# Layer-1 ConvFFN: an up projection as a 2x2 block product of seven products, then a separate down projection

## The chip, the cores and the metric

The kernel runs on one core of one Trainium2 chip. The metric is the device time of one execution in microseconds (us), given as the median of several runs. TensorE (PE) does the matmuls, VectorE (DVE), ScalarE (ACT) and GpSimd (POOL) work on tiles in SBUF and PSUM, and SyncE (SP) issues nearly all transfers from and to DRAM.

## The reference

A network of two layers on 1024 latent tokens and 256 context tokens with 1024 features: differential attention in layer 0, 2-D neighbourhood attention in layer 1, and behind each a gated convolutional FFN with 2816 hidden features. The FFN of layer 1 works on the 1024 latent tokens alone:

```python
def conv_ffn(t, w_up, w_conv, b_conv, w_down):
    u = t @ w_up                                   # 1024 -> 2 x 2816
    up = jnp.pad(u, ((0, 0), (1, 1), (0, 0)))
    acc = b_conv
    for tap in range(3):
        acc = acc + up[:, tap:tap + n] * w_conv[tap]
    a, g = jnp.split(acc, 2, axis=-1)
    return (jax.nn.silu(g) * a) @ w_down           # 2816 -> 1024
...
h2 = rmsnorm(x, norm_ffn[i]) * (1.0 + sc2) + sh2
x = x + g2 * conv_ffn(h2, ffn_up[i], ffn_conv[i], ffn_conv_b[i], ffn_down[i])
...
return rmsnorm(x, norm_out)
```

## The kernel before

Everything is float32. A matmul operand is kept as two rounded parts, high and low, and a product is three matmuls: high by high, high weight by low token, low weight by high token. Features lie on the 128 partitions, tokens on the free axis, so 1024 features are 8 chunks (kc) and 1024 tokens are two blocks of 512 columns, the width of one matmul and of one PSUM bank. H[b] is a pair of tiles, Hh and Hl, the normalised tokens of block b.

Weights come through one object, `W`. Its queue names every weight tile in the order of use, and `get()` keeps four of them made ahead. For each, `load` issues a 512 KB transfer into one of three raw tiles (line 106, on SP), lets POOL round it to the high part (`tensor_scalar`, L115) and subtract for the low part (`tensor_tensor`, L117), into one of five split slots (wsp). A slot is free again when its last matmul is done.

`wo_proj` (L397) is the output projection of the attention. At each block's end DVE adds it to the residual X (L406), ACT squares it (L298) and DVE sums the squares into SS (L299). `rnorm` (L302) makes the factor R of a block: eight matmuls on SS (L306), a root on ACT, a reciprocal, a product with the identity on DVE (L312), two matmuls that spread it (L315) and a copy on ACT (L316). `norm_mod` (L319) writes t, Hh and Hl from it (L328 DVE, L329 ACT, L330 DVE). The norm of block 1 is made inside the first up products.

`ffn(1, ...)` then goes over 22 units i of 128 hidden features. Per unit the up product takes two weight tiles, a and g, over both token blocks (`gemm`, L345): 2 x 8 chunks x 3 x 2 blocks = 96 matmuls. `conv` reads the sum u from PSUM: ACT makes the middle tap (L458), DVE the two others (L463); ACT makes the SiLU (L521), `gate` multiplies (DVE L471), rounds (ACT L472) and subtracts (DVE L473). The down product of an earlier unit is laid between the up products of the next ones: `down_step` takes 48 matmuls a unit (L488), and for every output chunk and block DVE adds the result to X in SBUF (L489). Each sum there is three matmuls, so L489 runs 16 times a unit, 352 in all. The last block's sums of squares and output are written at the end: `finish1`, `write`.

A scheduler sets the order on each engine from the program's order and its data dependences; no table of numbers touches this change.

## Time and profile before

| | us |
|---|---|
| median of 3 runs (lowest to highest) | 3350.94 (3348.80 to 3353.13) |
| the profiled execution, its own time | 3355.75 |
| its span, first to last instruction | 3354.0 |
| PE busy in it | 3234.7 |
| DVE busy | 2213.5 |
| POOL busy | 1169.2 |
| layer-1 FFN, first up to last down matmul | 2600.4 to 3335.6 |

The span is what lies between the first and the last instruction; the execution's own time lies 1.75 us over it. The rows below are cut from this one execution. In them a busy time is the sum over the instructions of an engine, "xN" is a count of instructions, and an arrow "<-" behind an idle time names what ended it. L numbers are lines of the kernel before.

### The profile page before, as it was taken

To read this page: it belongs to the slowest core of one execution; us is meant where nothing else is said; L and a number is where in the kernel's file an instruction comes from. 1 tells how busy PE (TensorE), PEld (TensorE's weight loads), DVE (VectorE), ACT (ScalarE), POOL (GpSimd) and SP (SyncE) were. 2 spreads that over 40 slices of the span, in tenths; PEclk is the share of its full clock that TensorE was granted. 3 is DMA by queue.
4 is the path that set the end of the run, shared out by engine and by line. 5 is a ranking of instruction groups with operands and counts; after the bars stand their busy time and mean duration, and the time that the engine had idled before them with its cause. 6 is when DMAs were issued, how large, how long until landed. Compare 5 with 4: busy or idle time off the path is not lost.

```text
span 3354.0 us, 42504 instructions
## 1 busy us (share of the span) xinstructions
PE 3234.7 (96%) x16160; PEld 2675.9 (80%) x16160; DVE 2213.5 (66%) x3647; ACT 1027.7 (31%) x1796; POOL 1169.2 (35%) x793
## 2 busy tenths in 40 slices
...
GB/s 261 160 210 169 126 112 106 114 116 71 142 69 52 46 55 44 52 50 51 51 38 38 32 116 262 238 126 199 198 157 100 48 42 57 44 51 51 44 44 51
DMA packets 165579, 334.60 MB, mean 100 GB/s; under 512 B 20352, under 2 KB 82176, under 8 KB 165376
## 3 DMA queue, kind: packets, MB, share of 16 engines
...
q8 instruction: 128, 2.10, 0.3%
...
## 4 chain that ended last, share of the span: by engine, by line
PE 68%; DVE 4%; ACT 1%; issue 1%; POOL 0%; DMA 0%; POOLq 0%; SPq 0%; DVEq 0%; ACTq 0%
PE u L345 32%; PE y_ps L488 16%; PE qk_ps L345 6%; PE wo_ps L345 4%; PE o L1149 2%; PE wo_ps L420 1%; PE v_ps L357 1%; PE v_ps L356 1%; PE v_ps L355 1%; PE s L1074 1%; PE tl L1101 1%; DVE t L328 1%; DVE Hl L330 1%; PE s L1077 1%; PE tl L1115 1%
## 5 line engine op out<-in xcount | busy, mean ns | idle before, releaser
L345 PE MATMUL u<-Hh,wsp 128*128 128x512 f32 (+1 forms) x3520 | 884.3, 371 | 2.3 <-ACT Hh L329 1.2
L489 DVE SCALAR_TENSOR_TENSOR X<-y_ps,mod,X 128x512 f32<-128x512 f32 (+1 forms) x864 | 593.8, 695 | 430.4 <-PE y_ps L488 429.6
L115 POOL TENSOR_SCALAR wsp<-raw 128x1024 fp32r<-128x1024 f32 (+1 forms) x217 | 234.3, 1087 | 1758.6 <-PE u L345 826.4
L345 PEld LDWEIGHTS u<-Hh,wsp 128*128 128x128 f32 x3520 | 634.8, 188 | 132.2 <-ACT Hh L329 2.1
L488 PE MATMUL y_ps<-Gh,wsp 128*128 128x512 f32 (+1 forms) x1744 | 631.3, 373 | 3.1 <-DVE X L489 1.9
L345 PE MATMUL u<-Hl,wsp 128*128 128x512 f32 (+1 forms) x1760 | 496.0, 370 | 0.7 <-DVE Hl L330 0.7
L117 POOL TENSOR_TENSOR wsp<-raw,wsp 128x1024 fp32r<-128x1024 f32 (+1 forms) x217 | 484.2, 2241 | 10.9
L458 ACT ACTIVATE acc<-u,c_ffn_conv 128x1024 f32<-128x1024 f32 (+2 forms) x134 | 127.2, 981 | 1125.1 <-PE u L345 1123.2
L488 PEld LDWEIGHTS y_ps<-Gh,wsp 128*128 128x128 f32 x1744 | 328.5, 188 | 72.2 <-DVE X L489 2.8
L345 PEld LDWEIGHTS u<-Hl,wsp 128*128 128x128 f32 x1760 | 310.7, 189 | 54.0 <-DVE Hl L330 1.0
L345 PE MATMUL qk_ps<-Hh,wsp 128*128 128x512 f32 (+1 forms) x1408 | 328.4, 364 | 0.0
L488 PE MATMUL y_ps<-Gl,wsp 128*128 128x512 f32 (+1 forms) x872 | 323.9, 371 | 0.0
L463 DVE SCALAR_TENSOR_TENSOR acc<-u,c_ffn_conv,acc 128x1023 f32<-128x1023 f32 (+2 forms) x268 | 256.9, 997 | 46.2 <-ACT acc L458 45.2
L345 PEld LDWEIGHTS qk_ps<-Hh,wsp 128*128 128x128 f32 x1408 | 239.2, 188 | 43.6
L276 DVE SCALAR_TENSOR_TENSOR ada<-raw,c_cvec,ada 128x512 f32<-128x512 f32 x224 | 169.8, 795 | 53.3 <-DMA raw<-in_ada_w_dram 52.0
L765 ACT ACTIVATE E<-E,st 128x1280 f32<-128x1280 f32 x128 | 175.3, 1369 | 68.6 <-DVE st L760 67.4
L775 POOL TENSOR_TENSOR E<-E,E 128x1280 f32<-128x1280 f32 x64 | 188.5, 2945 | 5.3
L345 PE MATMUL qk_ps<-Hl,wsp 128*128 128x512 f32 (+1 forms) x704 | 183.0, 363 | 0.0
L488 PEld LDWEIGHTS y_ps<-Gl,wsp 128*128 128x128 f32 x872 | 164.5, 189 | 18.4 <-issue 0.5
L760 DVE CUSTOM_DVE_ANT_0 E<-sl,zero,st 128x1024 f32<-128x1024 f32 x128 | 163.8, 1281 | 22.6 <-PE sl L758 22.1
L758 PE MATMUL sl<-kst,q 128*128 128x512 f32 x512 | 160.0, 436 | 1.6 <-DVE st L760 1.6
L809 PE MATMUL o<-T,vt 128*128 128x512 f32 (+1 forms) x464 | 154.7, 461 | 0.3 <-ACT ot L816 0.2
...
## 6 DMA issues: line engine op xcount, KB each, us to landing
...
q<-qscr SPq DMA_DIRECT2D x256, 64.0 KB
...
```

Of the source, the lines that this page charges most:

```text
L115: nc.gpsimd.tensor_scalar(out=sp[:, 0, c:c + n], in0=raw[:, c:c + n], scalar1=1.0, scalar2=1.0, op0=ALU.mult, op1=ALU.mult)
L117: nc.gpsimd.tensor_tensor(out=sp[:, 1, c:c + n], in0=raw[:, c:c + n], in1=f32(sp[:, 0, c:c + n]), op=ALU.subtract)
L276: stt(out=accs[v], in0=tv[:, kk, :], scalar=scol[:, kc, v:v + 1], in1=accs[v], op0=ALU.mult, op1=ALU.add)
L345: T.matmul(out=ps, lhsT=w[:, kc, :], rhs=H[b][s][:, kc, :], start=(kc == 0 and i == 0), stop=(kc == KC - 1 and i == 2))
L463: stt(out=acc[:, x0:x1], in0=u[:, x0 + d - t0:x1 + d - t0], scalar=w[:, tap:tap + 1], in1=acc[:, x0:x1], op0=ALU.mult, op1=ALU.add)
L488: T.matmul(out=y[:, :n], lhsT=w[:, j, :], rhs=g[:, b0 - g0:b0 - g0 + n], start=(i == 0), stop=(i == len(seq) - 1))
L489: stt(out=X[:, j, b0:b0 + n], in0=y[:, :n], scalar=mod[l][:, 40 + j, s:s + 1], in1=X[:, j, b0:b0 + n], op0=ALU.mult, op1=ALU.add)
L758: T.matmul(out=ps[:, 512 * c:512 * c + 512], lhsT=qs[2 * j + s][:, qc], rhs=ks[j][:, 512 * c:512 * c + 512], start=(s == 0), stop=(s == 1))
L760: V.tensor_tensor_reduce(out=E[j][:, :SEQ], in0=ps, in1=zero.broadcast_to([P, SEQ]), op0=ALU.add, op1=ALU.min, scale=-1.0, scalar=m, accum ...
L765: S.activation(out=E[j], in_=E[j], func=AF.Exp, scale=-1.0, bias=m, accum_out=sm)
L775: G.tensor_tensor(out=E[0], in0=E[0], in1=E[1], op=ALU.add)
L809: T.matmul(out=o[:, :n], lhsT=w, rhs=x, start=(i == 0 and j == 0), stop=(i == len(seq) - 1 and j == len(three) - 1))
```

## The change

The layer-1 FFN leaves `ffn` and is written anew in two phases. The residual X becomes one tile for each token block, and X after the output projection is also written to DRAM (`xspill`).

**Up.** For unit i the two weight tiles a and g, and the two halves of the 1024 features, make a 2x2 block matrix; the two halves of the features and the two token blocks make the other. Their product is made from seven block products (Strassen's scheme in Winograd's form) instead of eight. Each has 4 chunks x 3 matmuls = 12 matmuls of 512 columns, so a unit has 84. The weights need sums of blocks: `forms` makes four sums of 128x512 on POOL, three rounded copies on ACT and three low parts on POOL; the fourth weight tile, plain a, is split as before. The tokens need sums too: T1, T2, T3, T4 and B22, made once after the norm of block 1 (`token_forms`). Four units (NE = 4) have their two products on block 0 alone (`first`, `second`) ahead of these. The sums of products are made in PSUM where a bank can be accumulated further, and by five DVE additions of 512 columns (L1394, L1397, L1403, L1405, L1408), which write u into SBUF. `conv` reads u there. The gated values of 1024 tokens go to DRAM (`gscr`).

**Down.** Behind all up products, one token block after the other: eight PSUM banks hold the eight output chunks over all 22 units, gated values come back from DRAM and are split by ACT and DVE (L1292, L1293), and the down weights are loaded twice. DVE adds to X once a chunk and block (16 times, L1448). The output of block 0 is written during block 1.

```diff
+    def add_forms(self, a, g):
+
+        raw = []
+        for i in range(3):
+            self.todo.append(((i, a, g, raw), None))
...
+        if split is None:
+            yield from self.forms(*src)
+            return
...
+    def forms(self, i, a, g, raw):
+        nc = self.nc
+        if i == 0:
+            for x, src in enumerate((a, g)):
+                t = self.raw_pool.tile([P, 1024], F32, name=f"raw{self.count}_{x}", tag="raw")
+                nc.sync.dma_start(out=t, in_=src)
+                raw.append(t)
+            raw.append(self.sum_pool.tile([P, 1024], F32, name=f"sum{self.count}", tag="sum"))
+        n = (1024, 1024, 512)[i]
+        sp = self.split_pool.tile([P, 2, n], F32R, name=f"wf{self.count}", tag="wsp", padded_shape=[P, 2, 1024])
+        self.made.append((sp, 0))
+        ra, rg, s = raw[:3]
+        a1, a2, g1, g2 = ra[:, :512], ra[:, 512:], rg[:, :512], rg[:, 512:]
+        tt = nc.gpsimd.tensor_tensor
+        if i == 0:
+            tt(out=s[:, 512:], in0=g1, in1=g2, op=ALU.add)
+            tt(out=s[:, :512], in0=s[:, 512:], in1=a1, op=ALU.subtract)
+            src = s
+        elif i == 1:
+            tt(out=a1, in0=a1, in1=g1, op=ALU.subtract)
+            tt(out=a2, in0=a2, in1=s[:, :512], op=ALU.subtract)
+            src = ra
+        else:
+            src = g2
+        nc.scalar.copy(out=sp[:, 0, :], in_=src)
+        tt(out=sp[:, 1, :], in0=src, in1=f32(sp[:, 0, :]), op=ALU.subtract)
...
+            stt(out=X[b][:, j, :], in0=ps[:, :n], scalar=mod[l][:, 16 + j, s:s + 1], in1=xr[:, :n],
                 op0=ALU.mult, op1=ALU.add)
-            sumsq(np_, SS, X[:, j, b0:b0 + n], j, b0, n)
+            if l == 1:
+                nc.sync.dma_start(out=xspill[:, j, b0:b0 + n], in_=X[b][:, j, :])
...
+    for i in range(NE):
+        W.add(a["up"][1, i])
+    for i in range(NF):
+        if i >= NE:
+            W.add(a["up"][1, i])
+        W.add_forms(a["up"][1, i], a["up"][1, NF + i])
+    for _ in range(2):
+        for i in range(NF):
+            W.add(a["down"][1, i])
...
+    def split(form, kc, x, eng):
+        S.copy(out=form[:, kc, 0, :], in_=x)
+        eng.tensor_tensor(out=form[:, kc, 1, :], in0=x, in1=f32(form[:, kc, 0, :]), op=ALU.subtract)
...
+    def token_forms():
+
+        R = rnorm(yp, np_, SS, 512, 512)
+        tx = xpool.tile([P, KC, 512], F32, name="tx", tag="X0")
+        names = {"T1": hp, "T2": hp, "T3": (hp, "Hh1"), "T4": (hp, "Hl1"), "B22": (xpool, "X1")}
+        F = {}
+        for c in (0, 4, 1, 5, 2, 6, 3, 7):
+            stt(out=tx[:, c], in0=X[1][:, c, :], scalar=scale2[1][:, c, 0:1], in1=R, op0=ALU.mult, op1=ALU.mult)
+        for x, p in names.items():
+            p, tag = p if isinstance(p, tuple) else (p, x)
+            F[x] = p.tile([P, 4, 2, 512], F32R, name=f"F{x}", tag=tag)
+        b1, b2 = mod[1][:, 24:28, 0:1], mod[1][:, 28:32, 0:1]
+        V.tensor_tensor(out=bdiff, in0=b2, in1=b1, op=ALU.subtract)
+        twos = []
+        for kc in range(4):
+            x1, x2 = small(), small()
+            stt(out=x1, in0=tx[:, kc], scalar=b1[:, kc], in1=f32(H[0][0][:, kc, :]), op0=ALU.add, op1=ALU.subtract)
+            G.tensor_tensor(out=x1, in0=x1, in1=f32(H[0][1][:, kc, :]), op=ALU.subtract)
+            stt(out=x2, in0=tx[:, 4 + kc], scalar=b2[:, kc], in1=x1, op0=ALU.add, op1=ALU.subtract)
+            split(F["T2"], kc, x2, G)
+            split(F["T1"], kc, x1, V)
+            twos.append(x2)
+        for kc in range(4):
+            t1, t2 = tx[:, kc], tx[:, 4 + kc]
+            stt(out=t1, in0=t2, scalar=bdiff[:, kc], in1=t1, op0=ALU.add, op1=ALU.subtract)
+            split(F["T3"], kc, t1, G)
+        for kc in range(4):
+            t2 = tx[:, 4 + kc]
+            S.activation(out=F["B22"][:, kc, 0, :], in_=t2, func=AF.Identity, bias=b2[:, kc])
+            stt(out=F["B22"][:, kc, 1, :], in0=t2, scalar=b2[:, kc], in1=f32(F["B22"][:, kc, 0, :]),
+                op0=ALU.add, op1=ALU.subtract)
+        for kc in range(4):
+            x2 = twos[kc]
+            G.tensor_tensor(out=x2, in0=f32(H[0][0][:, 4 + kc, :]), in1=x2, op=ALU.subtract)
+            V.tensor_tensor(out=x2, in0=x2, in1=f32(H[0][1][:, 4 + kc, :]), op=ALU.add)
+            split(F["T4"], kc, x2, V)
+        return F
...
+    def product(ps, sp, c, form, start):
+        for kc in range(4):
+            h, l = (sp[:, s, (4 * c + kc) * P:(4 * c + kc + 1) * P] for s in range(2))
+            for i, (w, s) in enumerate(((h, 0), (h, 1), (l, 0))):
+                T.matmul(out=ps, lhsT=w, rhs=form(kc, s), start=(start and kc + i == 0), stop=(kc == 3 and i == 2),
+                         skip_group_check=not start)
+
+    def of(x):
+        return lambda kc, s: F[x][:, kc, s, :]
+
+    def first(aa):
+        x, p1 = bank(), np_.tile([P, 512], F32, name="p1", bufs=NE)
+        product(x, aa, 0, lambda kc, s: H[0][s][:, kc, :], True)
+        S.copy(out=p1, in_=x)
+        return x, p1
+
+    def second(x, aa):
+        product(x, aa, 1, lambda kc, s: H[0][s][:, 4 + kc, :], False)
...
+    def conv(u, acc, c):
+        w = convw[:, 1, c, :]
+        S.activation(out=acc, in_=u, func=AF.Identity, scale=w[:, 1:2], bias=w[:, 3:4])
+        stt(out=acc[:, 1:], in0=u[:, :-1], scalar=w[:, 0:1], in1=acc[:, 1:], op0=ALU.mult, op1=ALU.add)
+        stt(out=acc[:, :-1], in0=u[:, 1:], scalar=w[:, 2:3], in1=acc[:, :-1], op0=ALU.mult, op1=ALU.add)
+
+    bdiff = np_.tile([P, 4, 1], F32, name="bdiff")
+    early = []
+    for i in range(NE):
+        aa = W.get()
+        early.append((aa,) + first(aa))
+        if i == 0:
+            F = token_forms()
+    for aa, x, _ in early:
+        second(x, aa)
+    work = xpool.tile([P, 4, SEQ], F32, name="work", tag="X0")
+    ua, ug, acc_a, acc_g = (work[:, i] for i in range(4))
+    lo, hi = slice(0, 512), slice(512, 1024)
+    add = ALU.add
+    for i in range(NF):
+        if i < NE:
+            _, x, p1 = early[i]
+        else:
+            aa = W.get()
+            x, p1 = first(aa)
+        f = W.get()
+        y, u2 = bank(), small()
+        product(y, f, 0, of("T2"), True)
+        V.tensor_tensor(out=u2, in0=y, in1=p1, op=add)
+        z, q = bank(), small()
+        product(z, f, 1, of("T1"), True)
+        V.tensor_tensor(out=q, in0=z, in1=p1, op=add)
+        if i >= NE:
+            second(x, aa)
+        S.copy(out=ua[:, lo], in_=x)
+        f = W.get()
+        product(y, f, 0, of("T3"), False)
+        V.tensor_tensor(out=ug[:, hi], in0=y, in1=q, op=add)
+        product(z, f, 1, of("B22"), False)
+        V.tensor_tensor(out=ua[:, hi], in0=z, in1=u2, op=add)
+        f = W.get()
+        product(y, f, 0, of("T4"), False)
+        V.tensor_tensor(out=ug[:, lo], in0=y, in1=p1, op=add)
+        conv(ua, acc_a, i)
+        conv(ug, acc_g, NF + i)
+        S.activation(out=acc_g, in_=acc_g, func=AF.Silu)
+        V.tensor_tensor(out=acc_a, in0=acc_a, in1=acc_g, op=ALU.mult)
+        nc.sync.dma_start(out=gscr[i], in_=acc_a)
...
+    def load_g(n):
+        for _ in range(n):
+            if not loads:
+                return
+            b, k = loads.popleft()
+            if k % 4 == 0:
+                gs[b, k // 4] = hp.tile([P, 4, 2, 512], F32R, name=f"g{k // 4}", tag=gtags[k // 4])
+            t = small()
+            nc.sync.dma_start(out=t, in_=gscr[k][:, 512 * b:512 * b + 512])
+            split(gs[b, k // 4], k % 4, t, V)
...
+        def down(k, j, sp):
+            wh, wl = parts(sp)
+            g = gs[b, k // 4]
+            for i, (w, s) in enumerate(((wh, 0), (wh, 1), (wl, 0))):
+                T.matmul(out=ys[j], lhsT=w[:, j, :], rhs=g[:, k % 4, s, :], start=(k == 0 and i == 0),
+                         stop=(k == NF - 1 and i == 2))
+
+        def end(j):
+            xr = small()
+            nc.sync.dma_start(out=xr, in_=xspill[:, j, b0:b0 + 512])
+            x = xo[b][:, j, :]
+            stt(out=x, in0=ys[j], scalar=mod[1][:, 40 + j, 0:1], in1=xr, op0=ALU.mult, op1=ALU.add)
+            sumsq(np_, SS, x, j, b0, 512, V if j > 5 else G)
...
+        sps = [W.get() for _ in range(2)]
+        load_g(2)
+        for j in range(KC):
+            if b == 1 and j == 3:
+                Rs.append(rnorm(yp, np_, SS, 0, 512))
+            if j >= 6:
+                ys.append(yp.tile([P, 512], F32, name="y_ps", tag="y"))
+            for k in range(2):
+                down(k, j, sps[k])
+        if b == 1:
+            write(0, xo[0], Rs[0])
+        for k in range(2, NF - 3):
+            sp = W.get()
+            load_g(1)
             for j in range(KC):
...
-        last_norm = wo_proj(1, bp, pool, Th, (0, 1), H, SS, np_, yp)
...
-        ffn(1, up_, yp, pool, H, (0, 1), finish1, None, last_norm, yx)
...
+                down(k, j, sp)
+        sps = [W.get() for _ in range(3)]
+        load_g(3)
+        for j in range(KC):
+            for k in range(3):
+                down(NF - 3 + k, j, sps[k])
+            end(j)
+    write(1, xo[1], rnorm(yp, np_, SS, 512, 512))
```

What stands in the engines' queues. POOL in the middle of the up products, before, the splits of three weight tiles, as many as a unit has (a, g and down); wsp is the split slot, raw the loaded tile.

```order
L115 TENSOR_SCALAR wsp_25384<-raw_25382 128x1024
L117 TENSOR_TENSOR wsp_25384<-raw_25382,wsp_25384 128x1024
L115 TENSOR_SCALAR wsp_25389<-raw_25387 128x1024
L115 TENSOR_SCALAR wsp_25586<-raw_25584 128x1024
L117 TENSOR_TENSOR wsp_25389<-raw_25387,wsp_25389 128x1024
L117 TENSOR_TENSOR wsp_25586<-raw_25584,wsp_25586 128x1024
```

The same place after the change, one unit; sum holds the sums of weight blocks, wf is the slot of a weight form.

```order
L126 TENSOR_SCALAR wsp_23179<-raw_23177 128x1024
L128 TENSOR_TENSOR wsp_23179<-raw_23177,wsp_23179 128x1024
L147 TENSOR_TENSOR sum_23201<-raw_1_23199 128x512
L148 TENSOR_TENSOR sum_23201<-sum_23201,raw_0_23197 128x512
L151 TENSOR_TENSOR raw_0_23197<-raw_0_23197,raw_1_23199 128x512
L152 TENSOR_TENSOR raw_0_23197<-raw_0_23197,sum_23201 128x512
L157 TENSOR_TENSOR wf_23202<-sum_23201,wf_23202 128x1024
L157 TENSOR_TENSOR wf_23250<-raw_0_23197,wf_23250 128x1024
```

A ninth row, L157 on 512 columns, ends the unit. Where POOL had six rows of 1024 for a unit (its a, g and down tiles), it now has four of 1024 and five of 512 in the up phase.

DVE in the middle of the up products, before, around one gate; u and y_ps are in PSUM, acc, X, Gh and Gl in SBUF.

```order
L463 SCALAR_TENSOR_TENSOR acc<-u_24150,c_ffn_conv,acc 128x1023
L489 SCALAR_TENSOR_TENSOR X<-y_ps,mod_91,X 128x512 x14
L463 SCALAR_TENSOR_TENSOR acc<-u_24151,c_ffn_conv,acc 128x1023 x2
L471 TENSOR_TENSOR acc<-acc 128x1024
L473 TENSOR_TENSOR Gl<-acc,Gh 128x1024
```

And after, one unit; work holds u and the convolutions of both halves in SBUF, w_ps is a bank, p a saved first product.

```order
L1394 TENSOR_TENSOR t<-w_ps,p_23312 128x512
L1412 TENSOR_TENSOR work<-work 128x1024
L1397 TENSOR_TENSOR t<-w_ps,p_23312 128x512
L1403 TENSOR_TENSOR work<-w_ps,t 128x512
L1405 TENSOR_TENSOR work<-w_ps,t 128x512
L1369 SCALAR_TENSOR_TENSOR work<-work,c_ffn_conv 128x1023
L1408 TENSOR_TENSOR work<-w_ps,p_23312 128x512
L1370 SCALAR_TENSOR_TENSOR work<-work,c_ffn_conv 128x1023
L1369 SCALAR_TENSOR_TENSOR work<-work,c_ffn_conv 128x1023
L1370 SCALAR_TENSOR_TENSOR work<-work,c_ffn_conv 128x1023
```

The four taps (L1369, L1370) and the gate (L1412) now have all their tile inputs in SBUF; the gate stands behind the next unit's first addition.

POOL behind the norm of block 1, after the change; FT_22606 is T3, FT_22605 is T2, t a 512-column scratch tile. Before, only weight splits stood here.

```order
L1315 TENSOR_TENSOR t<-t,Hl_21959 128x512
L1293 TENSOR_TENSOR FT_22606<-tx,FT_22606 128x512
L147 TENSOR_TENSOR sum_22724<-raw_1_22722 128x512
L1293 TENSOR_TENSOR FT_22605<-t,FT_22605 128x512
L1315 TENSOR_TENSOR t<-t,Hl_21959 128x512
L1331 TENSOR_TENSOR t<-Hh_21958,t 128x512
L148 TENSOR_TENSOR sum_22724<-sum_22724,raw_0_22720 128x512
L157 TENSOR_TENSOR wf_22702<-raw_1_22560,wf_22702 128x512
```

Token forms and the weight sums of units 0 and 1 alternate in one queue; from the first of these rows to the fourth L1293 of T2 there are 22, two of them 128x1024.

DVE a little later, where the token forms end and unit 0 begins; FT_22604 is T1, FT_22607 is T4, p_22569 the first product of unit 0, and L1394 makes its u2.

```order
L1293 TENSOR_TENSOR FT_22604<-t,FT_22604 128x512
L1327 SCALAR_TENSOR_TENSOR FB_22608<-tx,mod_91,FB_22608 128x512
L1332 TENSOR_TENSOR t<-t,Hl_21959 128x512 x4
L1293 TENSOR_TENSOR FT_22607<-t,FT_22607 128x512 x4
L1394 TENSOR_TENSOR t<-w_ps,p_22569 128x512
L1397 TENSOR_TENSOR t<-w_ps,p_22569 128x512
```

The first addition of unit 0 stands behind all of T4.

## Rows read from the trace of the kernel before

**Rows 1.** The page: busy time of each engine over the span; data moved by slice.
```profile
PE 3234.7 (96%) x16160; PEld 2675.9 (80%) x16160; DVE 2213.5 (66%) x3647; ACT 1027.7 (31%) x1796; POOL 1169.2 (35%) x793
...
GB/s 261 160 210 169 126 112 106 114 116 71 142 69 52 46 55 44 52 50 51 51 38 38 32 116 262 238 126 199 198 157 100 48 42 57 44 51 51 44 44 51
```

**Rows 2.** Busy time by stretch, layer-1 FFN; the first line names the columns.
```profile
core 0: us, PE busy (x) PEld busy (x) DVE busy (x) ACT busy (x) POOL busy (x), PEclk, DMA share, GB/s
2600.40:2640.00 39.60, 33.67 (x135) 25.89 (x135) 28.43 (x35) 14.37 (x19) 10.64 (x6) 0.91 0.16 54
2700.00:3300.00 600.00, 600.00 (x2648) 496.98 (x2647) 371.17 (x401) 85.63 (x76) 187.12 (x109) 1.00 0.14 46
3300.00:3335.60 35.60, 32.69 (x144) 25.90 (x142) 18.80 (x28) 19.22 (x30) 16.87 (x13) 1.00 0.00 1
```

**Rows 3.** Waits of PE at start and end: total, times, longest.
```profile
PE rn_ps L306 <- DVE SS L299: 2.9, 1, 2.9
PE u L345 <- ACT Hh L329: 1.2, 1, 1.2
...
PE rn_ps L306 <- POOL SS L299: 4.0, 1, 4.0
PE rb_ps L315 <- DVE R L312: 3.5, 2, 1.8
```

**Rows 4.** Instructions by line, 2700 to 3300: busy us, mean ns | idle before.
```profile
L489 DVE SCALAR_TENSOR_TENSOR X<-y_ps,mod,X 128x512 f32<-128x512 f32 x288 | 214.2, 749 | 162.0 <-PE y_ps L488 162.0
...
L117 POOL TENSOR_TENSOR wsp<-raw,wsp 128x1024 fp32r<-128x1024 f32 x55 | 131.6, 2408 | 1.6
...
L463 DVE SCALAR_TENSOR_TENSOR acc<-u,c_ffn_conv,acc 128x1023 f32<-128x1023 f32 x75 | 95.9, 1279 | 23.5 <-ACT acc L458 22.8
L115 POOL TENSOR_SCALAR wsp<-raw 128x1024 fp32r<-128x1024 f32 x54 | 56.3, 1053 | 401.3 <-PE y_ps L488 319.7 <-PE u L345 81.5
...
L471 DVE TENSOR_TENSOR acc<-acc 128x1024 f32<-128x1024 f32 x19 | 44.0, 2316 | 22.6 <-ACT acc L521 22.6
L473 DVE TENSOR_TENSOR Gl<-acc,Gh 128x1024 fp32r<-128x1024 f32 x19 | 23.3, 1226 | 21.2 <-ACT Gh L472 21.2
```

**Rows 5.** Timeline 2893 to 2906: start, duration, instruction, [idle before].
```profile
2896.79 4.78 POOL L117 TENSOR_TENSOR wsp<-raw,wsp 128x1024 fp32r<-128x1024 f32 x2
...
2900.25 2.40 DVE L471 TENSOR_TENSOR acc<-acc 128x1024 f32<-128x1024 f32 x1 [1.19 <-ACT acc L521]
...
2903.77 1.23 DVE L473 TENSOR_TENSOR Gl<-acc,Gh 128x1024 fp32r<-128x1024 f32 x1 [1.12 <-ACT Gh L472]
```

**Rows 6.** Timeline of DVE, 2580 to 2630: the norm's operations in threes.
```profile
2589.61 4.99 DVE L330 SCALAR_TENSOR_TENSOR Hl<-t,mod,Hh 128x512 fp32r<-128x512 f32 x3
...
2619.95 2.07 DVE L330 SCALAR_TENSOR_TENSOR Hl<-t,mod,Hh 128x512 fp32r<-128x512 f32 x3
```

**Rows 7.** Timeline of POOL, 2580 to 2605: weight splits.
```profile
2581.70 1.05 POOL L115 TENSOR_SCALAR wsp<-raw 128x1024 fp32r<-128x1024 f32 x1 [23.67 <-PE wo_ps L345]
2582.83 2.40 POOL L117 TENSOR_TENSOR wsp<-raw,wsp 128x1024 fp32r<-128x1024 f32 x1
2589.82 1.46 POOL L115 TENSOR_SCALAR wsp<-raw 128x1024 fp32r<-128x1024 f32 x1 [4.58 <-PE wo_ps L345]
2591.36 2.71 POOL L117 TENSOR_TENSOR wsp<-raw,wsp 128x1024 fp32r<-128x1024 f32 x1
2595.26 1.60 POOL L115 TENSOR_SCALAR wsp<-raw 128x1024 fp32r<-128x1024 f32 x1 [1.19 <-PE wo_ps L345]
```

**Rows 8.** Timeline 2606 to 2620: the norm of token block 1.
```profile
2611.41 1.84 PE L306 MATMUL rn_ps<-mean_w,SS 128*128 128x2 f32 x8 [2.86 <-DVE SS L299]
...
2617.34 0.59 ACT L316 COPY R<-rb_ps 128x512 f32<-128x512 f32 x1 [3.79 <-PE rb_ps L315]
```

**Rows 9.** Timeline 3330 to 3354: last sums and the output.
```profile
3333.20 2.64 POOL L299 TENSOR_TENSOR SS<-SS,sq 128x512 f32<-128x512 f32 x2 [1.04 <-ACT sq L298]
...
3336.42 14.09 SPq L1256 DMA_DIRECT2D out_dram<-X  x16
...
3337.92 1.58 POOL L299 TENSOR_TENSOR SS<-SS,sq 128x512 f32<-128x512 f32 x1 [2.08 <-ACT sq L298]
```

105 lines of the change are left out of this document (57 added, 48 removed).

## The prediction

> **What bounds the kernel now.** I read the busy shares of the page first: TensorE (PE) is busy for 96% of the span, VectorE (DVE) 66%, GpSimd (POOL) 35% [rows 1]. A share over the whole span says nothing of one stage, so next came busy time by stretch for the layer-1 ConvFFN, which runs from 2600.4 us (last output-projection matmul) to 3335.6. In its middle 600 us PE is busy for all 600.0, with 2648 matmuls at the full granted clock: 600 / 2648 = 0.2267 us a matmul [rows 2]. The reader should see that nothing but matmul count matters there. Its two ends differ. The first 39.6 us hold 135 matmuls, worth 30.6, so 9.0 are lost; the last 35.6 hold 144, worth 32.6, so 3.0 are lost. The waits name the losers: sums of squares and the normalised tokens at the start, the norm's own chain at the end [rows 3]. After the last matmul come 18.4 us of norm and output.
>
> Then, because the change hands work to POOL and DVE, I looked at what these two do in the middle: POOL rounds weights to a high part (1.05 us per 128x1024) and subtracts for the low part (2.41), 31% busy, otherwise waiting for a slot that PE frees; DVE evicts [rows 4]. One row there is odd: L471 and L473 do the same kind of operation on the same size, two inputs in SBUF, and take 2.32 and 1.23. In the timeline L471 starts at 2900.25 during a POOL subtraction and ends at 2902.65, 1.08 after the subtraction's end at 2901.57; L473 comes when POOL is idle [rows 5]. At 2589.61 and 2619.95 the same is seen on 512 columns: three L330 take 4.99 beside POOL and 2.07 without [rows 6]. POOL pays as well: beside those operations its L117 takes 2.71 instead of 2.40 and its L115 1.46 instead of 1.05 [rows 7]. L463 and L489, with one input in PSUM, keep their time (1.28, 0.75) beside the same POOL work [rows 4]. So a DVE operation that reads two SBUF operands and a POOL operation do not overlap here, and each makes the other wait.
>
> **What goes.** The up product of a unit falls from 96 to 84 matmuls; 22 units save 264, 264 x 0.2267 = **-59.8**. The down product keeps its 1056. DVE loses 352 L489 of 0.75, which lay beside PE, so they bring nothing by themselves.
>
> **The up loop, per unit** (18 units, i = 4 to 21). PE needs 84 x 0.2267 = 19.04. POOL gets one plain split (1.05 + 2.41), two low parts of 1024 (2 x 2.41), and five two-input operations of 512, which took 1.32 on POOL (two in 2.64) [rows 9]: taken as 1.30, 6.50. With nine gaps of 0.08 [rows 7] that is 15.5. Alone it fits under 19.04. But DVE now has five operations per unit with both inputs in SBUF: four convolution taps (u now comes from SBUF) and the gate. Each keeps POOL waiting. The rows price this on 512 columns at 0.30 to 0.55; the 1024-column operation is 0.54 longer (1.23 against 2.07 / 3 = 0.69), so 0.84 to 1.09. Eight of POOL's nine are subtractions and sums like L117, whose delay is the 0.30, so I take 0.86: 15.5 + 5 x 0.86 = 19.8, more than PE. Bounds: zero, if POOL's slack meets it; 1.08 each, if POOL waits out DVE's operation as DVE waits out POOL's, 20.9. With 19.8, nearest to the measured POOL delays: 18 x 0.76 = **+13.7** (0 to 33.5). DVE itself: five PSUM adds at 0.75, five SBUF operations at 1.23, with four or five waits of 1.2 to 2.4 is 15 to 20, about the same limit. ScalarE's seven operations are under 10 us and wait for nobody else.
>
> On this the Trainium skill, page "SBUF — State Buffer", section "Who interferes with whom", says that a DVE instruction with two SBUF inputs contends with a GpSimd instruction that reads SBUF, and that it is an exclusive lock: whoever issues first has it, the other fully blocks. The trace agrees for DVE (it ends 1.08 after POOL); for POOL a wait of only 0.30 beside a 0.69 operation is shown. By the page's rule the loop would stand at 20.9.
>
> **The start.** Times from 2600.4. PE has 96 matmuls that need only block 0 (21.8 us). Before, the sums reached PE at +11.0 [rows 8]; now POOL also makes unit 0's four weight sums meanwhile, and DVE's remaining additions wait for them: +15. The norm's factor follows 6.5 later (2611.4 to 2617.9), so the token forms begin at +22. POOL by then works through two plain splits (6.9), four sums (5.2), two low parts (4.8), gaps and DVE's holds (7): free at +24 to +25. Its queue now holds 22 rows until T2, the first form that PE needs, is whole: 20 of 512 and 2 of 1024 are 26.0 + 4.8 = 30.8, with gaps 1.7 and some 17 DVE holds of 0.30 (5.1) making 38. T2 is whole at +62. In the DVE queue u2 of unit 0 (L1394), which frees the bank for the T3 product, stands behind eight operations for T4, alternating with POOL: 8 x 1.3 to 1.6, so it is done near +75. PE has issued 120 matmuls by then (27.2). The other 216 of units 0 to 3 need 49.0, and DVE makes 2 us a unit more of it: +132 against 336 x 0.2267 = 76, a loss of **+56**. Bounds: 33 without any blocking (T2 at +53, u2 at +60), 70 with POOL held for DVE's full time. Before's 9.0 at this place go: **-9.0**. In such idle stretches the granted clock falls (0.91 mean in the first 39.6 us [rows 2]); PE then waits anyway, so I price it at zero.
>
> **Down.** 44 units of 24 matmuls are 5.4 us each; POOL splits one in 3.5, DVE and ACT split one gate tile in about 1.3. It loads 0.75 MB per unit, 0.14 MB a us: over what the middle moves now (46 GB/s), under the 262 that the page shows in another stretch [rows 1]. Hidden. Where up ends, unit 21 passes through the gate, DRAM and a split while PE has no other work: its convolution, SiLU, gate, store and load cover five loads issued ahead, so only the banks' evictions stand in the way: +2 (0 to 8). The norm of block 0 now lies inside down: +1.5. The stalls of before at the end go: **-3.0**. In the tail eight outputs go out instead of sixteen and the last sum is on DVE (0.69 against POOL's 1.58 [rows 9]): **-2**.
>
> **Sum:** -59.8 + 13.7 + 56 - 9.0 + 2 + 1.5 - 3.0 - 2 = -0.6, against the profiled execution's 3355.75. That execution lies 4.8 over the median of the three, so the change is put on the median: 3350.94 - 0.6 = **3350**.
>
> **Rivals.** (B) *The blocking costs less than the rows suggest.* For it: the priced waits come from stretches in which POOL had slack to spare around them, and a POOL operation may take a gap that DVE leaves. The loop then goes at PE's 19.04 (0) and the start loses about 44; with the rest of the sum as it is (-9.0 + 2 + 1.5 - 3.0 - 2 = -10.5) that is -59.8 + 44 - 10.5 = -26, **3325**, from 3314 (start 33) to 3340 (start 56, loop 3). Against it: POOL and DVE are both busy over 80% of every unit. (C) *Slower: POOL is held for the whole DVE operation* and becomes the bound of the loop. The place is POOL's weight forms in the loop; it decides from the point where the holds pass 19.04 - 15.5 = 3.5 us a unit (0.7 an operation), and at 1.08 an operation costs 33.5 instead of 13.7; with the start at 61 that is -59.8 + 33.5 + 61 - 10.5 = +24, **3375**. For it: DVE's own waits are exactly of this kind [rows 5]. Against it: the 0.30 [rows 7]. It is what the full block of the Trainium skill's page named above would come to. (D) *The change pays in full*: the start covered by the 96 early matmuls and the loop on PE, -59.8 - 10.5 = -70, 3281. Against it: 30.8 us of POOL work alone stand between the norm and T2, and the early matmuls last 21.8. It is the far end of B.
>
> **How the numbers follow.** Two executions of this kernel lie some 0.2% apart, so a difference under 0.2% (6.7 us, 3344 to 3358) can't be told from none. Near the sum, 3340 to 3360: 0.40, of which 0.30 within the 0.2% and the rest evenly at either side. B: 0.33, of which 0.02 within. C: 0.25, of which 0.01 within. D: 0.02. That makes faster 0.05 + 0.31 + 0.02 = 0.38, same 0.33, slower 0.05 + 0.24 = 0.29. The 8-in-10 range takes in B but for its far end, and C to its middle and a little over: **3315 to 3378**; the likeliest case's own is 3340 to 3360.
>
> **What the profile after would show.** PE should still have 0.2267 a matmul in the down phase, with over 430 matmuls per 100 us; in the loop 84 matmuls per 19.8 us (19.0 for B, 20.9 for C); about 120 matmuls in the first 75 us after the output projection. POOL should be busy without a gap over 0.2 us from there to the end of up, its 512-column rows longer than 1.3 where DVE is beside it, and convolution taps (L1369, L1370) and the gate over 2 us. The prediction is wrong if taps take 1.2 us beside a busy POOL, if PE waits for transfers in down, or if the first T2 product starts near +50.

## The result and the profile after

The changed kernel takes 3372.17 us, the kernel before 3351.99 (medians of four runs each): the ratio is 1.0061, with a 95% interval of 1.0044 to 1.0079. It is slower by 20.2 us, where the likeliest forecast was 3350 and no change. The profiled execution of after has 3369.63 us of its own time and a span of 3367.7, that of before 3355.75 and 3354.0. So the two traces explain 13.7 us; the other 6.5 lie in how these two executions stand to their medians (before's 3.8 over, after's 2.5 under).

The first view is busy time by stretch, from the last matmul of the output projection to the last of the down products. The columns are those of [rows 2].

```profile
core 0: us, PE busy (x) PEld busy (x) DVE busy (x) ACT busy (x) POOL busy (x), PEclk, DMA share, GB/s
2598.80:2634.00 35.20, 26.75 (x106) 21.18 (x104) 22.48 (x23) 10.55 (x18) 14.77 (x9) 0.85 0.21 68
2634.00:2681.00 47.00, 17.33 (x38) 9.96 (x36) 41.07 (x26) 13.21 (x21) 44.81 (x27) 0.60 0.11 34
...
2740.00:3080.00 340.00, 338.09 (x1479) 276.56 (x1478) 244.90 (x175) 124.46 (x140) 332.58 (x156) 1.00 0.32 108
3080.00:3102.00 22.00, 15.03 (x55) 11.25 (x55) 14.87 (x14) 7.01 (x10) 14.58 (x8) 0.84 0.68 218
3102.00:3230.00 128.00, 128.00 (x567) 105.98 (x566) 45.83 (x34) 18.62 (x30) 88.52 (x50) 1.00 0.44 148
3230.00:3250.00 20.00, 13.55 (x53) 10.73 (x52) 10.31 (x13) 7.96 (x15) 4.07 (x3) 0.83 0.56 192
3250.00:3351.80 101.80, 101.80 (x450) 83.97 (x448) 37.09 (x26) 14.03 (x22) 69.55 (x39) 1.00 0.38 128
```

A matmul still costs what it did, 0.2267 us (128.0 / 567 = 0.2257, 101.8 / 450 = 0.2262), so each row tells its loss: its length less its matmuls at that price. The loop's row: 340 - 1479 x 0.2267 = 4.7. The row at 3080, 22 - 55 x 0.2267 = 9.5, is the passage from up to down. The row at 3230 holds ten matmuls of the norm; 20 - 43 x 0.2267 = 10.3 is lost between the token blocks. The rest, some 69, is lost before 2745. In the kernel before, the same place had 135 matmuls in 39.6 us [rows 2]. Counted exactly, by when the nth matmul after the output projection starts, less n x 0.2267, the ledger of the two profiled executions follows. Tail is the time from the start of the last matmul to the end.

| term | forecast us | measured us |
|---|---|---|
| 264 matmuls fewer | -59.8 | -59.9 |
| start, up to the 336th matmul | +56 | +69.3 |
| the same place before | -9.0 | -11.6 |
| the up loop, 18 units | +13.7 | +5.0 |
| from up to down | +2 | +9.8 |
| between the two token blocks | +1.5 | +10.6 |
| late stalls of before | -3.0 | -5.1 |
| tail after the last matmul | -2 | -2.6 |
| all ahead of the FFN | 0 | -1.8 |
| sum | -0.6 | +13.7 |

The longest waits of PE over the stretch name the places (total, times, longest); SS holds the sums of squares, FT the token forms, t a scratch tile with u2 or q:

```profile
PE rn_ps L347 <- DVE SS L340: 17.2, 3, 8.4
PE w_ps L1351 <- DVE t L1394: 15.1, 14, 6.3
PE w_ps L1351 <- POOL FT L1293: 13.4, 3, 5.9
...
PE w_ps L1351 <- DVE work L1403: 5.4, 1, 5.4
```

All waits of PE there come to 65.9 us, the four losses of the ledger to 94.7. Most of the rest is matmuls that ran slow: in the 47 us in which the token forms are made the mean granted clock is 0.60, and 38 matmuls take 17.33 us, 0.46 each, 8.7 more than at 0.2267. The other places of this kind follow below.

**The loop.** One unit on POOL, from one L126 to the next, in the timeline (start, duration, instruction):

```profile
2881.48 2.02 POOL L126 TENSOR_SCALAR wsp<-raw 128x1024 fp32r<-128x1024 f32 x1
2883.59 3.25 POOL L128 TENSOR_TENSOR wsp<-raw,wsp 128x1024 fp32r<-128x1024 f32 x1
2886.79 2.28 POOL L147 TENSOR_TENSOR sum<-raw 128x512 f32<-128x512 f32 x1
2889.15 2.32 POOL L148 TENSOR_TENSOR sum<-sum,raw 128x512 f32<-128x512 f32 x1
...
2896.42 4.63 POOL L157 TENSOR_TENSOR wf<-raw,wf 128x1024 fp32r<-128x1024 f32 x2
2901.03 2.03 POOL L126 TENSOR_SCALAR wsp<-raw 128x1024 fp32r<-128x1024 f32 x1
```

Its period is 2901.03 - 2881.48 = 19.55, beside 19.8 forecast and PE's 19.04. Five operations are lengthened against their prices of before [rows 4, 9]: 2.02 for 1.05, 3.25 for 2.41, 2.28 and 2.32 for 1.30, and one of the last pair, 4.63 for 3.71. That is 4.7 us, 0.84 to 1.02 each, and it makes up the period with POOL's own 14.8.

DVE in the same unit:

```profile
2882.52 2.06 DVE L1369 SCALAR_TENSOR_TENSOR work<-work,c_ffn_conv 128x1023 f32<-128x1023 f32 x1
2884.61 3.30 DVE L1370 SCALAR_TENSOR_TENSOR work<-work,c_ffn_conv 128x1023 f32<-128x1023 f32 x1
2887.84 0.68 DVE L1394 TENSOR_TENSOR t<-w_ps,p 128x512 f32<-128x512 f32 x1
2889.10 1.23 DVE L1412 TENSOR_TENSOR work<-work 128x1024 f32<-128x1024 f32 x1 [0.58 <-ACT work L1411]
...
2896.88 3.01 DVE L1369 SCALAR_TENSOR_TENSOR work<-work,c_ffn_conv 128x1023 f32<-128x1023 f32 x1 [1.84 <-ACT work L1368]
```

The taps take 1.7 to 3.3 us. The gate L1412 starts 0.05 us ahead of POOL's L148 and takes only 1.23; there POOL is the one that waits. Up to unit 10 PE goes at 19.04 us a unit although POOL's period is 19.4 to 19.6 already: the first weight form of a unit is ready 6.0 us before PE needs it in unit 5, half a microsecond less in each later one, and from unit 11 on 3.1. From there PE loses 0.5 us a unit. It waits then not for the weight form but, by 0.2 us, for the addition L1394 behind the held taps.

**The start.** POOL between the norm and T2, in the timeline; the bracket is idle time before and what ended it:

```profile
2627.41 2.59 POOL L157 TENSOR_TENSOR wf<-raw,wf 128x1024 fp32r<-128x1024 f32 x1 [17.86 <-ACT wf L156]
2631.29 1.29 POOL L1315 TENSOR_TENSOR t<-t,Hl 128x512 f32<-128x512 f32 x1 [1.29 <-DVE t L1314]
...
2637.16 1.71 POOL L1293 TENSOR_TENSOR FT<-t,FT 128x512 fp32r<-128x512 f32 x1
...
2667.21 1.72 POOL L1293 TENSOR_TENSOR FT<-t,FT 128x512 fp32r<-128x512 f32 x1
```

DVE in the same stretch, from the norm's factor to u2 of unit 0:

```profile
2623.02 7.53 DVE L1305 SCALAR_TENSOR_TENSOR tx<-X,scale,R 128x512 f32<-128x512 f32 x8 [3.89 <-ACT R L357]
...
2642.24 1.75 DVE L1293 TENSOR_TENSOR FT<-t,FT 128x512 fp32r<-128x512 f32 x1
...
2680.67 0.68 DVE L1394 TENSOR_TENSOR t<-w_ps,p 128x512 f32<-128x512 f32 x1
```

For most of the time from 2634 to 2669 the two engines go in step, 1.71 for POOL's 1.30 and 1.75 for DVE's 0.69. POOL's 22 rows take 37.6 us, 38 forecast. But they begin at +32.7 from the output projection's end (2598.6), not at +24. Two things hold them. POOL itself is free only at 2630.0 (+31.4), because its last weight form waited 17.86 us for ScalarE's rounding L156, and that for a split slot which PE frees behind the norm. And their first operand comes at 2631.2, behind the eight scaled tiles on DVE.

PE's first row behind u2 of unit 0, and busy time from there to the 336th matmul (columns as above):

```profile
2681.40 4.45 PE L1351 MATMUL w_ps<-FT,wf 128*128 128x512 f32 x12 [6.29 <-DVE t L1394]
...
2681.40:2744.30 62.90, 54.49 (x206) 43.42 (x207) 41.90 (x34) 22.48 (x23) 36.45 (x19) 0.87 0.22 75
```

The 206 matmuls are worth 46.7 us. So 8.4 us are lost to waits for DVE's first additions, and 7.8 to matmuls that run slow behind them.

**From up to down.** SyncE, DVE and PE in the timeline:

```profile
3087.86 0.33 SPq L1413 DMA_DIRECT2D gscr<-work  x1
3088.24 2.71 SPq L1428 DMA_DIRECT2D t<-gscr  x5
...
3093.59 2.65 DVE L1293 TENSOR_TENSOR g<-t,g 128x512 fp32r<-128x512 f32 x2 [5.15 <-ACT g L1292]
...
3096.16 0.68 DVE L1403 TENSOR_TENSOR work<-w_ps,t 128x512 f32<-128x512 f32 x1
...
3096.89 4.89 PE L1351 MATMUL w_ps<-FT,wf 128*128 128x512 f32 x12 [5.37 <-DVE work L1403]
```

The reloads of gated tiles stand on SyncE behind the store of unit 20. Their splits (L1293) stand in DVE's queue ahead of the last unit's addition L1403, and PE waits for that. Its twelve matmuls then take 4.89 us, where a row of twelve takes 2.88 at the full granted clock (at 2891.43). By the ledger's count 2.1 of the 9.8 us are lost ahead of this wait, at the additions behind the last held gate, 5.7 in it and 2.0 in the twelve.

**Between the blocks.** SyncE, DVE and PE in the timeline, where block 0 ends and block 1 begins:

```profile
3224.65 0.33 SPq L117 DMA_DIRECT2D raw<-in_down_dram  x1
3225.02 0.43 SPq L1446 DMA_DIRECT2D t<-xspill  x1
...
3228.97 0.75 DVE L1448 SCALAR_TENSOR_TENSOR X<-y_ps,mod,t 128x512 f32<-128x512 f32 x1 [10.80 <-DMA t<-xspill]
...
3233.30 0.38 SPq L1446 DMA_DIRECT2D t<-xspill  x1
...
3239.70 1.87 PE L347 MATMUL rn_ps<-mean_w,SS 128*128 128x2 f32 x8 [6.45 <-DVE SS L340]
3241.43 4.34 PE L1441 MATMUL y_ps<-g,wsp 128*128 128x512 f32 x12
```

Two of the eight residual reloads (L1446) go out only when a weight load ahead of them has found a free raw tile. DVE's eviction waits 10.8 us for one, the sums are late, and PE, in whose queue the norm of block 0 stands 18 matmuls into block 1, waits 6.45; the twelve matmuls behind it take 4.34 us instead of 2.88.

### The profile page after: what moved, and what is told of

Its sections match the earlier page's. It is cut to its first block, busy times and chain, and to the rows that moved or that the text cites. A ratio compares the mean times of both kernels' runs of the same rounds, so it can differ in the third digit from the quotient of the medians.

```text
span 3367.7 us, 42589 instructions
## 1 busy us (share of the span) xinstructions
PE 3196.9 (95%) x15896; PEld 2635.7 (78%) x15896; DVE 2204.4 (65%) x3480; ACT 1118.6 (33%) x1938; POOL 1542.4 (46%) x959
## 4 chain that ended last, share of the span: by engine, by line
PE 59%; DVE 7%; issue 3%; POOL 2%; ACT 2%; DMA 1%; SPq 0%; DVEq 0%; ACTq 0%; POOLq 0%
PE u L386 18%; PE y_ps L531 9%; PE w_ps L1351 7%; PE y_ps L1441 6%; PE qk_ps L386 6%; PE wo_ps L386 4%; PE o L1203 2%; DVE work L1369 2%; PE wo_ps L463 1%; PE v_ps L398 1%; PE v_ps L397 1%; PE v_ps L396 1%; PE tl L1155 1%; PE s L1128 1%; DVE work L1370 1%
## 5 line engine op out<-in xcount | busy, mean ns | idle before, releaser
L126 POOL TENSOR_SCALAR wsp<-raw 128x1024 fp32r<-128x1024 f32 (+1 forms) x217 | 259.9, 1202 | 1347.4 <-PE u L386 705.4
L128 POOL TENSOR_TENSOR wsp<-raw,wsp 128x1024 fp32r<-128x1024 f32 (+1 forms) x217 | 508.1, 2347 | 13.3
L386 PE MATMUL u<-Hh,wsp 128*128 128x512 f32 (+1 forms) x2112 | 502.7, 357 | 0.0
L533 DVE SCALAR_TENSOR_TENSOR X<-y_ps,mod,X 128x256 f32<-128x256 f32 (+1 forms) x528 | 344.3, 661 | 235.3 <-PE y_ps L531 234.5
L386 PEld LDWEIGHTS u<-Hh,wsp 128*128 128x128 f32 x2112 | 370.0, 189 | 73.2 <-issue 0.8
L531 PE MATMUL y_ps<-Gh,wsp 128*128 128x512 f32 (+1 forms) x1040 | 361.8, 362 | 2.2 <-DVE X L533 1.5
L1351 PE MATMUL w_ps<-FT,wf 128*128 128x512 f32 x1056 | 268.8, 409 | 44.2 <-DVE t L1394 15.1
L1351 PEld LDWEIGHTS w_ps<-FT,wf 128*128 128x128 f32 x1056 | 206.2, 197 | 98.9 <-DVE t L1394 21.0
L386 PE MATMUL u<-Hl,wsp 128*128 128x512 f32 (+1 forms) x1056 | 276.4, 357 | 0.0
L1441 PE MATMUL y_ps<-g,wsp 128*128 128x512 f32 x1056 | 241.7, 391 | 0.0
L1441 PEld LDWEIGHTS y_ps<-g,wsp 128*128 128x128 f32 x1056 | 199.2, 189 | 41.9 <-issue 0.5
L808 ACT ACTIVATE E<-E,st 128x1280 f32<-128x1280 f32 x128 | 175.3, 1369 | 68.6 <-DVE st L803 67.4
L531 PE MATMUL y_ps<-Gl,wsp 128*128 128x256 f32 (+1 forms) x520 | 187.2, 360 | 0.5 <-DVE Gl L516 0.5
```

Source lines behind the costliest of these rows:

```text
L126: nc.gpsimd.tensor_scalar(out=sp[:, 0, c:c + n], in0=raw[:, c:c + n], scalar1=1.0, scalar2=1.0, op0=ALU.mult, op1=ALU.mult)
L128: nc.gpsimd.tensor_tensor(out=sp[:, 1, c:c + n], in0=raw[:, c:c + n], in1=f32(sp[:, 0, c:c + n]), op=ALU.subtract)
L386: T.matmul(out=ps, lhsT=w[:, kc, :], rhs=H[b][s][:, kc, :], start=(kc == 0 and i == 0), stop=(kc == KC - 1 and i == 2))
L531: T.matmul(out=y[:, :n], lhsT=w[:, j, :], rhs=g[:, b0 - g0:b0 - g0 + n], start=(i == 0), stop=(i == len(seq) - 1))
L533: stt(out=x, in0=y[:, :n], scalar=mod[l][:, 40 + j, s:s + 1], in1=x, op0=ALU.mult, op1=ALU.add)
L808: S.activation(out=E[j], in_=E[j], func=AF.Exp, scale=-1.0, bias=m, accum_out=sm)
```

## The experiments

Three theories were tried. **Theory 1:** the losses in the down phase come from the order of SyncE's and DVE's queues. **Theory 2:** POOL's list with DVE's holds sets the start and the loop. **Theory 3:** in the start, the five split slots keep POOL idle. The rivals are in the expectations. Losses are counted as in the ledger, from one profiled execution each; changes of time are against the changed kernel's 3372.17. Executions of one kernel spread over 4 to 8 us, and in the traces the output projection, which no edit touches, ends anywhere between 2598.6 and 2603.4 us. So a difference of 2 or 3 us in the time says nothing, and the losses say more than the time.

| run | us | ratio to before | start | loop | up to down | between blocks | tail |
|---|---|---|---|---|---|---|---|
| changed kernel | 3372.17 | 1.0061 | 69.3 | 5.0 | 9.8 | 10.6 | 16.3 |
| e2_xr_act | 3376.37 | 1.0075 | 69.8 | 5.5 | 10.5 | 4.6 | 27.5 |
| e3_g_pool | 3365.86 | 1.0043 | 68.3 | 5.0 | 3.7 | 11.5 | 16.7 |
| e4_tf_dve | 3362.99 | 1.0033 | 57.9 | 5.9 | 10.2 | 10.8 | 17.1 |
| e6_no_sums | 3340.68 | 0.9966 | 49.2 | 0.0 | 4.5 | 11.1 | 17.1 |
| e10_xr_first | 3364.46 | 1.0043 | 68.1 | 5.0 | 9.3 | 2.9 | 18.2 |
| e11_norm_after | 3365.96 | 1.0052 | 63.8 | 5.0 | 10.7 | 11.2 | 17.4 |
| e13_all_b | 3345.65 | 0.9984 | 55.0 | 4.9 | 4.0 | 2.9 | 16.9 |
| e12_all | 3336.62 | 0.9963 | 54.3 | 0.5 | 0.0 | 2.9 | 16.8 |
| e14_ne3 | 3331.25 | 0.9947 | 50.8 | 0.4 | 0.0 | 2.9 | 17.2 |
| e14_ne2 | 3334.16 | 0.9954 | 54.3 | 0.3 | 0.0 | 2.9 | 15.9 |

**Residual reloads on ScalarE's queue.**

```diff
-            nc.sync.dma_start(out=xr, in_=xspill[:, j, b0:b0 + 512])
+            nc.scalar.dma_start(out=xr, in_=xspill[:, j, b0:b0 + 512])
```

> The 16 reloads of the residual in the down phase (L1446) are issued from ScalarE's queue instead of SyncE's. Theory 1 (queue order): two of block 0's reloads stood behind weight loads that waited for a raw tile, so the last sums of block 0 reached PE late, and PE lost 10.6 us there. Then that loss falls to 1 to 3 us and the time by 7 to 9 us. Rival (the last eviction, square and sum of block 0 are simply too late for a norm placed 18 matmuls into block 1, whatever the queue): the loss stays at 8 or more and the time within 3 us of the changed kernel.

The loss between the blocks fell from 10.6 to 4.6, less than expected, and the time rose by 4.2 us. The tail says why; timeline at its end:

```profile
3359.70 0.63 ACT L339 ACTIVATE sq<-X 128x512 f32<-128x512 f32 x1 [2.28 <-DVE X L1448]
3359.76 0.33 ACTq L1446 DMA_DIRECT2D t<-xspill  x1
...
3362.60 0.75 DVE L1448 SCALAR_TENSOR_TENSOR X<-y_ps,mod,t 128x512 f32<-128x512 f32 x1 [1.47 <-DMA t<-xspill]
```

On ScalarE a reload stands behind the square of the chunk before, and the square waits for the eviction that waits for its reload: a ring of 3.6 to 4.3 us a chunk, and a tail of 27.5 us. So it is the order in a queue that counts, but this edit changes one order for another and doesn't settle the first.

**Residual reloads first.**

```diff
-NS = 7
+NS = 8
...
-            xr = small()
-            nc.sync.dma_start(out=xr, in_=xspill[:, j, b0:b0 + 512])
+            xr = xrs[j]
...
-        sps = [W.get() for _ in range(3)]
         load_g(3)
+        xrs = [small() for _ in range(KC)]
+        for j in range(KC):
+            nc.sync.dma_start(out=xrs[j], in_=xspill[:, j, b0:b0 + 512])
+        sps = [W.get() for _ in range(3)]
```

> The eight residual reloads of a block are issued from SyncE again, but all of them ahead of the block's last three weight loads (eight scratch tiles instead of seven). Theory 1 (queue order on SyncE): PE's loss between the blocks falls from 10.6 us to 2 or 3, and the tail stays at 16 to 17 us, since no reload waits for ScalarE's square of the chunk before as in the run with ScalarE's queue: the time falls by 7 to 9 us. Rival (the place of the norm sets it): the loss stays at 8 or more.

The loss fell to 2.9 and the time by 7.7 us, both as theory 1 has it; the norm is at the same place in PE's queue, and the rival falls. The edit also adds a scratch tile and moves three gated reloads ahead; what these bring by themselves was not measured. Timeline of PE between the blocks:

```profile
3227.43 1.05 PE L347 MATMUL rn_ps<-mean_w,SS 128*128 128x2 f32 x8 [0.25 <-DVE SS L340]
3228.35 2.99 PE L1441 MATMUL y_ps<-g,wsp 128*128 128x512 f32 x12
```

The wait of 6.45 is 0.25, and the twelve matmuls behind it take 2.99 us instead of 4.34.

**First gate splits on POOL.**

```diff
-            split(gs[b, k // 4], k % 4, t, V)
+            split(gs[b, k // 4], k % 4, t, G if b == 0 and k < 7 else V)
```

> The low parts of the first seven reloaded gate tiles are made by POOL instead of DVE, so that none of them stands in DVE's queue ahead of the last unit's additions (L1403). Theory 1 (queue order): PE's 9.8 us loss between up and down falls to 3 or 4, the time by 5 to 7 us. Rival (the last gate blocked for 3.3 us by POOL, and the way through DRAM, set that gap): the loss stays at 8 or more, or grows since POOL has seven more operations.

The loss from up to down fell to 3.7, the time by 6.3 us. DVE at the place:

```profile
3084.90 3.30 DVE L1412 TENSOR_TENSOR work<-work 128x1024 f32<-128x1024 f32 x1 [0.59 <-ACT work L1411]
3088.12 0.68 DVE L1397 TENSOR_TENSOR t<-w_ps,p 128x512 f32<-128x512 f32 x1
3088.90 0.69 DVE L1403 TENSOR_TENSOR work<-w_ps,t 128x512 f32<-128x512 f32 x1
```

The gate L1412 takes 3.30 us, held by POOL as in the changed kernel (3.29), and L1403 follows at once all the same. So DVE's order was the cause of most of the gap, 7.7 of 9.8 us. The rival, the held gate, has the other 2.1, which are lost in this run as before; of the rest of its 3.7, 0.8 is PE's wait for POOL's splits. In e12_all this gate takes 1.23 us, and nothing is lost there.

**Token forms without POOL.**

```diff
-            G.tensor_tensor(out=x1, in0=x1, in1=f32(H[0][1][:, kc, :]), op=ALU.subtract)
+            V.tensor_tensor(out=x1, in0=x1, in1=f32(H[0][1][:, kc, :]), op=ALU.subtract)
...
-            split(F["T2"], kc, x2, G)
+            split(F["T2"], kc, x2, V)
...
-            split(F["T3"], kc, t1, G)
+            split(F["T3"], kc, t1, V)
...
-            G.tensor_tensor(out=x2, in0=f32(H[0][0][:, 4 + kc, :]), in1=x2, op=ALU.subtract)
+            V.tensor_tensor(out=x2, in0=f32(H[0][0][:, 4 + kc, :]), in1=x2, op=ALU.subtract)
```

> The 16 token-form operations that POOL has behind the norm (L1315, two kinds of L1293, L1331) go to DVE; POOL keeps the weight forms. Theory 2 (the two engines alternate in one chain, each operation stretched to 1.7 us): T2 is whole near +50 us after the output projection instead of +70, u2 of unit 0 near +65 instead of +82, PE's loss at the 336th matmul falls from 69 to 50 to 55, the time by 14 to 19 us. Rival (DVE's own list is the bound, and 16 more operations lengthen it): u2 at +82 or later, the loss the same or larger.

Sixteen more operations on DVE, and u2 of unit 0 came at +73.0 instead of +82.1; the start's loss is 57.9, the time 9.2 us less. The direction is theory 2's, the size two thirds of it. Three rows of DVE show it beside POOL and alone:

```profile
2644.27 2.82 DVE L1322 SCALAR_TENSOR_TENSOR tx<-tx,bdiff 128x512 f32<-128x512 f32 x1
2647.01 2.83 DVE L1293 TENSOR_TENSOR FT<-t,FT 128x512 fp32r<-128x512 f32 x1
2649.77 0.68 DVE L1315 TENSOR_TENSOR t<-t,Hl 128x512 f32<-128x512 f32 x1
```

Beside POOL's 1024-column weight forms an operation takes 2.83, without them 0.68: the weight forms, which stay on POOL, still hold DVE, and that part of the expected gain is not had.

**Weight sums left out.**

```diff
-            tt(out=s[:, 512:], in0=g1, in1=g2, op=ALU.add)
-            tt(out=s[:, :512], in0=s[:, 512:], in1=a1, op=ALU.subtract)
-            src = s
+            src = rg
...
-            tt(out=a1, in0=a1, in1=g1, op=ALU.subtract)
-            tt(out=a2, in0=a2, in1=s[:, :512], op=ALU.subtract)
```

> The four sums of weight blocks in each unit are left out; the rounded copies and low parts are made of the unsummed tiles, so POOL has five operations a unit instead of nine, 5.2 us less. Theory 2 (blocking of POOL by five DVE operations a unit sets the loop, 15.5 + 4.0 = 19.5 against PE's 19.0): POOL then needs about 14.3, the loop goes at 19.04, its loss of 5 us is gone; at the start four operations of 1.7 fewer stand before T2, loss 69 to 60 or 62: the time falls by 11 to 14 us. Rival (POOL's list is not the bound, DVE's additions and taps are): the loop stays at 19.5 and the start gains under 3 us.

This kernel leaves the sums out and so does not make the network's result; its time is a price of the sums, not a gain to be had. The loop's loss is 0.0, as theory 2 has it. The start gained 20 us where 7 to 9 were expected, and the passage from up to down 5.3 that nobody expected; the time fell by 31.5. u2 came at +69.7, 12.4 earlier, and the units 0 to 3 behind it lost 9.0 where they lose 17.1. POOL's sums cost more than their own length there. ScalarE's rounding has to wait for them too, but which wait brings how much of the 20 is left open.

**The norm placed later.**

```diff
         early.append((aa,) + first(aa))
-        if i == 0:
-            F = token_forms()
-    for aa, x, _ in early:
+    for i, (aa, x, _) in enumerate(early):
         second(x, aa)
+        if i == 0:
+            F = token_forms()
```

> The norm of block 1 is placed behind the first second-half product instead of behind the first first-half product in program order, so that PE has some 50 early matmuls ahead of its matmuls on the sums instead of 36, and the first split slot comes free earlier. Theory 3 (PE's queue and the five split slots hold POOL: it sat idle for 17.9 us waiting for the slot of the first weight tile): POOL's weight form starts 6 to 10 us earlier, PE's loss at the 336th matmul falls from 69 to 60 to 65, the time by 4 to 9 us. Rival (theory 2 alone: from the norm on, the alternating token forms are the chain, and PE's early matmuls only move within their cover): loss 67 to 70, time within 3 us.

As theory 3 has it: the weight form that waited 17.86 us starts at 2616.80 instead of 2627.41, the loss is 63.8, the time 6.2 us less. PE's matmul on the sums no longer stands ahead of the product that frees the slot. POOL's token rows begin 6 us later here, at +38.7, and u2 still comes 2.5 us earlier, at +79.6: POOL had done weight forms in the meantime, so it is its whole list that counts and not the start of the 22 rows.

**All together, without and with the rounding on ScalarE.** The second adds to the first:

```diff
-            nc.gpsimd.tensor_scalar(out=sp[:, 0, c:c + n], in0=raw[:, c:c + n], scalar1=1.0, scalar2=1.0,
-                                    op0=ALU.mult, op1=ALU.mult)
+            if self.on_act:
+                nc.scalar.copy(out=sp[:, 0, c:c + n], in_=raw[:, c:c + n])
+            else:
+                nc.gpsimd.tensor_scalar(out=sp[:, 0, c:c + n], in0=raw[:, c:c + n], scalar1=1.0, scalar2=1.0,
+                                        op0=ALU.mult, op1=ALU.mult)
...
+    W.on_act = True
...
+    W.on_act = False
     load_g(NG)
```

> Four edits together: reloads first, token forms on DVE, first gate splits on POOL, norm placed later. If the four losses lie behind each other on PE's time and not beside each other, their gains add: 8 (reloads) + 11 (forms) + 6 (gate splits) + what the norm's place brings (0 to 8): 25 to 33 us less than the changed kernel, 3339 to 3348, so 0 to 0.4% under the kernel before. Rival (the start's gains overlap, and POOL's gate splits collide): less than 18 us, slower than the kernel before.

> As the run before, and the high part of plain a in layer 1's up phase is made by ScalarE instead of POOL: POOL has 1.05 us less a unit, ScalarE 1.05 more (under 12 of 19). Theory 2 (POOL's list and its holds set the loop at 19.5): the loop goes at 19.04 or nearly, its loss of 5 us goes, and the start gains 2 to 4: 5 to 9 us below the run before. Rival (DVE's chain with its waits sets the loop): within 2 us of it.

Four edits brought 26.5 us, at the low end of 25 to 33: the two edits of the start gain 14.3 together where they gain 11.4 and 5.5 alone. The fifth brought 9.0 more. By the losses that is 4.4 in the loop, 4.0 from up to down, which the expectation does not name, and 0.7 at the start, where it has 2 to 4. The loop's loss fell to 0.5 with DVE's operations as before; POOL's period is PE's there, and POOL waits 1.76 us a unit for ScalarE. With the lead that runs out in the changed kernel this shows POOL's list as the loop's bound. In this kernel (e12_all) the timeline shows the norm's first eight operations on DVE as one row:

```profile
2625.78 14.67 DVE L1310 SCALAR_TENSOR_TENSOR tx<-X,scale,R 128x512 f32<-128x512 f32 x8 [3.38 <-ACT R L361]
```

14.67 us for what took 7.53 in the changed kernel, because POOL, idle there until 2627.41, makes weight forms beside nearly all of them here. What theory 3 won is in part given back through theory 2.

**Fewer early units.**

```diff
-NE = 4
+NE = 3
```

and NE = 2.

> The five edits of the last run, with three units whose products on block 0 come first instead of four (NE = 3). Theory 3 (the five split slots: each early unit holds one until its second product, and ScalarE's and POOL's weight forms wait for a slot, 50.8 us of POOL's waits in the first 160 us): forms of unit 0 and 1 start earlier, PE's loss at the 336th matmul falls from 54 to 45 to 51, the time by 3 to 8 us. Rival (cover: PE has 24 early matmuls fewer, 5.4 us, while the token forms are made): the loss grows by up to 5 us, time 0 to 5 us longer.

> The same with two early units (NE = 2). Theory 3: loss at the 336th matmul 40 to 50, the time 3 to 12 us less than with four. Rival (cover): 10.9 us of early matmuls fewer, loss up by 5 to 11 us.

Three units: loss 50.8 and 5.4 us less than with four, both inside theory 3's ranges. Two: loss 54.3, as with four, and 2.5 us less, which the spread of the executions covers; neither theory 3's 40 to 50 nor the rival's rise by 5 to 11 came. The traces show two opposite moves: u2 comes at +70.7, +67.4 and +63.4 with four, three and two units, and what is lost behind it is 13.5, 10.6 and 15.4. With NE = 3 the kernel takes 3331.25 us, 0.9947 of the kernel before (0.9933 to 0.9962), faster than both.

## Why the prediction was wrong

**Saved matmuls and their price:** right, -59.9, 0.2267 at both ends.

**The up loop:** right in mechanism, high in size. The taps are held by POOL, and taps and gate hold it in turn. The hold was priced at 0.86 from the waits of [rows 7] and is 0.84 to 1.02, 0.95 in the mean; POOL's gaps of 0.08, which I added nine times, are under 0.1 together. The two errors go opposite ways, so that the period, 19.55 instead of 19.8, comes out nearer than its parts. The term is 5.0 and not 18 x 0.5 because POOL's lead covered the first units: there is no loss between the 336th matmul and unit 11. The gate over 2 us, which the prediction names as a sign, did not come: it takes 1.23 and POOL waits.

**The start:** +69.3 for +56, the largest miss. The alternation itself was right (37.6 us for 38). The first step that failed is that POOL is free at +24 to +25 and its 22 rows then begin. POOL was free at +31.4, since it had stood idle for 17.86 us behind a weight form without a slot; and the eight scaled tiles on DVE, 7.5 us, for which the sum has no term, held the rows until +32.7. The norm's factor was late too, at +24.4 for +22: DVE waited some 2 us for each of the two last reloads of the residual, so the sums reached PE at +17.5 instead of +15. u2 came at +82.1 instead of +75. But PE had issued 132 matmuls by then, not 120, so 52.1 us were lost there instead of 47.8, which is 4.3 of the 13.3. The other 9.0 lie behind u2, in the second step that failed, "DVE makes 2 us a unit more of it": units 0 to 3 lost 17.1, not 8. About half of that is PE's waits for DVE's first additions, 8.4 us. In the trace DVE's taps wait there for ScalarE's L1368, and that stands in ScalarE's queue behind roundings that wait for slots or sums; e11 and e14_ne3, where slots come free earlier, lose 14.1 and 10.6, but how much the slots alone bring is open. The other half is the clock.

**The clock:** priced at zero because "PE then waits anyway". It does not hold where PE's products are themselves on the chain: behind u2 of unit 0 matmuls that ran slow cost 7.8 us, and after the two waits of the down phase twelve matmuls at a granted clock of 0.50 to 0.74 took 4.89 and 4.34 instead of 2.88.

**From up to down and between the blocks:** +2 and +1.5 became 9.8 and 10.6, so these steps missed by 16.9 together, more than the whole difference of the profiled executions, 13.7. Both steps were costed by engine time and transfer rate and left out the queues: what SyncE and DVE had ahead of the operation that PE waits for. That "only the banks' evictions stand in the way" is the step that failed between up and down; the +1.5 for the norm inside down was given without a reason. e3 and e10 show what stood there.

**The sum** missed by 14.3 us. The start, the two places of the down phase and the loop missed by +13.3, +16.9 and -8.7; the rest, -7.2, are before's own losses and small terms. That the miss is no larger is in part luck: the lead in the loop, which no term had, hides some of the others.

**The rivals.** C ended at 3375, next to what came, but not by its mechanism: its loop costs 33.5 and the measured one 5.0. POOL's hold, 0.95, lies between the forecast's 0.86 and C's 1.08. B's zero loop appears only when POOL has less to do (e6, e12). The range held the time only by the part that C brought to it, and C's mechanism did not come; the forecast named no change where the kernel is slower.

**The Trainium skill,** page "SBUF — State Buffer", section "Who interferes with whom", names the two-input operations and the exclusive lock. The traces agree: DVE's additions with a PSUM input keep 0.68 beside a busy POOL, the two-input ones behind a running POOL operation take 1.7 to 3.3, and the gate, which starts first, keeps 1.23 and POOL waits. A full block of POOL for 1.23 is not shown; the longest hold in the rows is 1.02.
